# A hybrid decoder layer on one core: two accumulator tiles for each Strassen pair, weight casts 100 instructions sooner, and B and C of two groups computed as pairs

## The chip, the core and the metric

The kernel runs on one core of a Trainium2 chip. The metric is the device time of one execution in microseconds, and the median of several executions is what counts. The core's engines each work through their own queue of instructions in the order in which the program puts them: PE (TensorE: matmuls; PEld is its weight loads), DVE (VectorE), ACT (ScalarE), POOL (GpSimd, which here mostly issues DMAs and tiny copies) and SP (SyncE, which issues DMAs). They wait for each other through semaphores. An instruction whose wait isn't over holds up everything behind it on its engine.

## The reference, cut to what matters

One layer: a projection of the normalised input, a pooling branch and a Mamba-2 scan merged by gates, then an MLP. There are 512 tokens and 16 meta tokens ahead of them, so 528 positions, and 1024 channels. The lines that the change bears on:

```python
u = rmsnorm(h, mix_norm_w[i])
proj = u @ w_in[i]
u_pool = proj[..., OFF_POOL:OFF_Z]
z = proj[..., OFF_Z:OFF_XBC]
xbc = proj[..., OFF_XBC:OFF_DT]
...
xbc = jax.nn.silu(causal_depthwise_conv(xbc, conv_w, conv_b))
xs = xbc[..., :D_INNER]                                   # 8 groups of 256 columns
b_mat = xbc[..., D_INNER:D_INNER + SSM_GROUPS * D_STATE]  # 8 groups of 128
c_mat = xbc[..., D_INNER + SSM_GROUPS * D_STATE:]         # 8 groups of 128
...
y = ssd_chunked(xs, dt, a, b_mat, c_mat) + xs * d_skip[:, None]
y = y * jax.nn.silu(z)        # then a norm for each group, and w_ssd_out
```

So each of the eight groups of the scan needs two column blocks of x, one of B, one of C and two of z, each 128 columns wide: six products of a 1024 x 128 weight block with u.

## The kernel before, in words

**Numbers.** Every product is made in three passes, because each operand is split into a rounded high part and the remainder: high x high, high x low, low x high. For a weight block of 128 x 1024 numbers in float32 (`raw`), ACT casts it to `whi` (L111) and DVE subtracts to get `wlo` (L113); both stand in `block_split`. There are four buffers each for `whi` and `wlo`, and three for `raw` (one more of another pool during the scan). `block` (L115) allots the tiles, has SP load the block (`block_load`, L95) and splits it.

**A plain projection** (`proj`, L207, called by `plain` and `z_half`) multiplies the block with u: for x, B and C in two column runs of 264 (258 for C, whose leading positions aren't needed), 48 matmuls; for z and the gates 24 matmuls of 512 columns. `plain` accumulates in a tile of `psum2`, which has two buffers of two banks each; `conv` (L433) then reads it with one operation of ACT and three of DVE, and ends with a Silu on ACT.

**A pair** (`pair`, L492) computes two column blocks together in the Strassen-Winograd form: seven products of quarter blocks (`MULTIPLY`: `b11`, `b21`, `t2`, `t1`, `s3`, `b22`, `t4`), of 12 matmuls with 264 columns each, 84 in all, where two plain blocks need 96. Products `b11`, `t2`, `s3`, `t4` accumulate in the first bank, one on top of the other, `b21`, `t1`, `b22` in the second. After each product its state is copied or added to the raw result `r` in SBUF (L510 to L524, ACT and DVE by turns), and `conv` reads `r`. Before the change both banks are the halves of one `psum2` tile. The weights for four of the products are sums of quarter blocks; they are made beforehand in DRAM by POOL's DMAs, some of which add (`weight_steps`, L768). A set of sums covers two pairs. `pair_operands` (L471) loads two quarter products into one `raw` tile at a time and splits it with `block_split`, so a pair needs three and a half blocks' worth of casts and subtractions where two plain blocks need two. The right operands are sums of parts of u, made once by `sums_of_u` during groups 0 to 3. Before the change x is made as a pair in groups 4 to 7 (`X_PAIRS`), and B and C nowhere (`BC_PAIRS = ()`). A branch for B and C as pairs with z between them stands in `group_proj` and in the host's `_weight_blocks` under the name `both`, and is not taken.

**The weave.** `weave` (L728) writes the program for group g by turns: a step of the scan of group g (`ssd`, L590), a step of the projections of group g + 1 (`group_proj`, L529), a step of `sums_of_u` and a step of `weight_sums_at`, which issues one of POOL's DMAs behind a small copy of what was just written (`mark`). While group 4 is scanned, the first part of the output product (`out_half`) is woven in; beside group 7's scan runs `out_part`. In three weaves a gate (`gate_pool`) comes between x and z.

**The order.** The order of writing isn't the order of issue. A planner goes through the program with a model of the times and gives each engine, whenever it is free, the ready instruction that was written first. `tc.issue_after(x)` puts an instruction behind x on its engine; `tc.high_priority(100)` ranks the instructions written under it as if they had been written 100 instructions sooner. Tiles of a pool are handed out in the course of the plan: an instruction that needs a buffer waits for the release of the one before, by all its readers. The small accumulators `psum1` (four of one bank) serve the scan (`ptb`, `ptm`, `ptx`, `pcb`, `pst`, `po`, `py`, `png`); the two `psum2` tiles serve the projections.

**Sets of sums.** `sets` (L760) is the list of weight sums to make: first those of the pairs (`fx`, 8 DMAs each), then those of the MLP (`f1` with 8 DMAs, `f2` with 4). `SETS_AT` says how many sets each group's weave takes from the list; what is left is made behind the loads of `ht` (L1188), before the MLP.

Of the kernel before, what the change touches and what calls it, by code (L numbers as in the profile page):

```python
# [11 lines left out]
AF = mybir.ActivationFunctionType  # L12
# [4 lines left out]
SEQ = 512  # L17
NM = 16
L = SEQ + NM
HALF = L // 2  # L20
# [27 lines left out]
SUMS_AT = range(4)  # L48

X_PAIRS = (4, 5, 6, 7)  # L50
BC_PAIRS = ()
PAIRS = [(k, g) for g in range(G) for k in "bx" if g in (BC_PAIRS if k == "b" else X_PAIRS)]

SETS_AT = {0: 1, 1: 1, 2: 2, 3: 1, 4: 2, 5: 2, 6: 1, 7: 1}
# [10 lines left out]
def kernel(ctx: ExitStack, tc, xT, x, w, fx, f1, f2, vec, fnw, out):  # L65
    nc = tc.nc
    act, dve, pe, pool = nc.scalar, nc.vector, nc.tensor, nc.gpsimd
# [13 lines left out]
    def raw_tile(name):  # L81
        nraw[0] += 1
        if scan_raw and nraw[0] % 4 == 0:
            return scan_raw[0].tile([P, 1024], F32, tag="raw", name=name)
        return wp.tile([P, 1024], F32, tag="raw", name=name, bufs=3)
# [8 lines left out]
    def block_load(t, c):  # L94
        nc.sync.dma_start(t[1][:, c], w[t[0], :, c])  # L95
# [5 lines left out]
    def after(*ins):  # L101
        st = ExitStack()
        for i in ins:
            if i is not None:
                st.enter_context(tc.issue_after(i.ins))
        return st

    def block_split(t, c, behind=None, cast_behind=None):
        b, raw, hi, lo = t
        with after(cast_behind):  # L110
            act.copy(hi[:, c], raw[:, c])  # L111
        with tc.issue_after(behind.ins) if behind is not None else nullcontext():
            dve.tensor_tensor(lo[:, c], raw[:, c], hi[:, c].bitcast(F32), op=ALU.subtract)  # L113

    def block(behind=None, cast_behind=None):  # L115
        t = block_tiles()
        block_load(t, slice(0, 1024))
        block_split(t, slice(0, 1024), behind, cast_behind)
        return t[2:]

    def raw_block():
# [70 lines left out]
    def psum2(name):  # L192
        return psa.tile([P, 1024], F32, tag="mm", name=name)
# [55 lines left out]
    b = nblk[0]  # L249
# [102 lines left out]
    for i in range(2):  # L352
        pb = psum1(f"pb1_{i}")
        c = slice(3 * i, 3 * i + 3)
# [14 lines left out]
    for c in range(4):  # L369
        r = slice(c * H, (c + 1) * H)  # L370
# [19 lines left out]
    for c in (slice(0, P), slice(P, W)):  # L390
        n = c.stop - c.start
# [39 lines left out]
    x_ready, z_ready, filled = {}, {}, {}  # L431
# [39 lines left out]
    def pair_operands(i):  # L471

        s, h = divmod(i, 2)
        q = {"b11": B11, "b22": B22, "b21": B21}
        for a in range(0, 7, 2):
            ms = [m[0] for m in MULTIPLY[a : a + 2]]
            n = nblk[1]
            nblk[1] += 1
            raw = raw_tile(f"rawp{n}")
            hi = wp.tile([P, 1024], F32R, tag="whi", name=f"whip{n}")  # L480
            lo = wp.tile([P, 1024], F32R, tag="wlo", name=f"wlop{n}")
            for j, m in enumerate(ms):
                src = fx[s, q[m]] if m in q else wsum["fx", s, m]
                nc.sync.dma_start(raw[:, 512 * j : 512 * (j + 1)], src[:, 512 * h : 512 * (h + 1)])
            c = slice(0, 512 * len(ms))
            block_split((n, raw, hi, lo), c)
            for j in range(len(ms)):
                yield hi[:, 512 * j : 512 * (j + 1)], lo[:, 512 * j : 512 * (j + 1)]

    second_product, halved = {}, {}  # L490

    def pair(kind, g, r):  # L492

        ps = psum2(f"pq{kind}{g}")
        banks = (ps[:, :HALF], ps[:, 512 : 512 + HALF])
        operands = pair_operands(PAIRS.index((kind, g)))
        one, two = HF
        for m, f, n, start, stop in MULTIPLY:
            o = banks[n]
            wt = next(operands)  # L500
            f = factor_u(f)
            for low in range(2):
                for k in range(4):
                    wk = wt[low][:, k * P : (k + 1) * P]
                    at = pe.matmul(o, wk, f[k][0], start=start and not low and k == 0,  # L505
                                   stop=stop and low == 1 and k == 3, skip_group_check=True)
                    if not low:
                        pe.matmul(o, wk, f[k][1], start=False, stop=False, skip_group_check=True)
            if m == "b11":
                act.copy(r[0][:, one], o)  # L510
            elif m == "b21":
                dve.tensor_tensor(r[0][:, one], r[0][:, one], o, op=ALU.add)
            elif m == "t2":
                second_product[g] = at
                act.activation(r[1][:, one], o, AF.Copy, scale=-1.0)
            elif m == "t1":
                act.copy(r[1][:, two], o)
                yield
            elif m == "s3":
                dve.tensor_tensor(r[1][:, two], r[1][:, two], o, op=ALU.subtract)  # L520
            elif m == "b22":
                dve.tensor_tensor(r[1][:, one], r[1][:, one], o, op=ALU.add)
            else:
                act.copy(r[0][:, two], o)  # L524
# [4 lines left out]
    def group_proj(g, cur, gate=None):  # L529

        first = g == 0
        xc, bt, ct, zt = cur

        def plain(dst, t, skip):
            if first and (dst is bt or dst is ct):
                view = viewB if dst is bt else viewC
            else:
                runs, view = wide(psum2(f"px{g}_{t}"), skip)
                proj(runs, block(), X if first else U)
            conv(dst, first_raw(t, view, skip) if first else view, t)  # L540

        def z_half(ps, i):

            with tc.issue_after(done[0].ins) if g == 1 else nullcontext():
                wt = block(None, halved.get(g - 1) if gate is not None else None)
            proj(narrow(ps), wt, X if first else U, None if i else second_product.get(g))

        bcs = ((bt, 16 + g, 0), (ct, 24 + g, NM - 4))
        xs = ((xc[:, 0, :], 2 * g, 0), (xc[:, 1, :], 2 * g + 1, 0))
        both = g in BC_PAIRS  # L550
        for kind, ts, paired in (("b", bcs, both), ("x", xs, g in X_PAIRS)):
            if paired:
                r = raw_pair(kind, g)
                yield from pair(kind, g, r)
                for (dst, t, skip), src in zip(ts, r):
                    conv(dst, src[:, skip:], t)
                yield
            else:
                for t in ts:
                    plain(*t)  # L560
                    filled.setdefault(g - 1, mm[0])
                    yield
            if both:
                i = 0 if kind == "b" else 1
                ps = psum2(f"pz{g}_{i}")[:, :SEQ]
                z_half(ps, i)
                z_ready[g] = act.activation(zt[:, i, :], ps, AF.Silu)
                yield
        if both:
            return  # L570
        if gate is not None:
            gate_pool(gate)
            yield
        ps = psum2(f"pz{g}")
        for i in range(2):
            z_half(ps[:, i * SEQ : (i + 1) * SEQ], i)
        zf = zt.rearrange("p i t -> p (i t)")
        if first:
            dve.tensor_tensor(zt, ps.rearrange("p (i t) -> p i t", i=2),
                              rsb[:, NM:].unsqueeze(1).to_broadcast([P, 2, SEQ]), op=ALU.mult)  # L580
            z_ready[g] = act.activation(zf, zf, AF.Silu)
        else:
            z_ready[g] = act.activation(zf, ps, AF.Silu)
        yield
# [465 lines left out]
    for d in range(NK):  # L1050
        ps = psum1(f"psl{d}")
# [108 lines left out]
    for n, d in enumerate(MERGE):  # L1160
# [9 lines left out]
        ps = psum2(f"pup{d}")[:, :SEQ]  # L1170
# [389 lines left out]
    for c in range(NC - 1):  # L1560
        z, e = c == 0, c == NC - 2

        n = 2 * c + 3
        a = ff1_plain(n, (range(4), range(4, NK))) if n < PLAIN else ff1_pair(n)
        b = ff1_pair(n + 1) if n + 1 < 16 else iter(())
# [61 lines left out]
    c = NC - 1  # L1627
# [14 lines left out]
    for t in range(4):  # L1642
        T, st = t // 2, slice((t % 2) * P, (t % 2 + 1) * P)
        n = 0
        for half in range(2):
            parts = [(0, 512)] if half == 0 or t < 3 else [(0, 256), (256, 256)]
            for a, m in parts:
                ps = p2v[t] if T == 0 and half == 0 else lastp[:, 512:] if a else (
                    lastp[:, :512] if (t, half) == (3, 0) else psum1(f"pl{t}_{half}"))
                ps = ps[:, a : a + m]  # L1650
                i = 0
# [4 lines left out]
                for k, seg in ((1, (A11, 3)[T]), (0, (A12, A22)[T])):  # L1656
                    wh, wl = wq[k, half]
                    for p in range(2):
                        x0 = p * 512 + a
                        f = i == 0 and not (T == 0 and half == 0) and not a  # L1660
# [18 lines left out]
def _weight_blocks(i):  # L1679
# [14 lines left out]

    def group(g, gate_d=None):
        z = lambda j: put(cols(w_in, OFF_Z + (2 * g + j) * P))
        both = g in BC_PAIRS
        for i, ts in enumerate(((16 + g, 24 + g), (2 * g, 2 * g + 1))):
            if g not in (X_PAIRS if i else BC_PAIRS):
                for t in ts:  # L1700
                    put(cols(w_in, OFF_XBC + t * P))
            if both:
                z(i)
        if gate_d is not None:
            gate(gate_d)
        if not both:
            for j in range(2):
                z(j)

    def wg(b):  # L1710
        put(w_g[2 * b : 2 * b + 2].reshape(2, 2, P, 256).transpose(2, 0, 1, 3).reshape(P, 1024))
# [119 lines left out]
```

## Time and profile before

| | us |
|---|---|
| median of three runs | 1015.87 (1014.68 to 1016.35) |
| the profiled execution, its own time | 1013.97 |
| its span in the trace | 1012.3 |
| PE busy | 992.1 |
| DVE busy | 804.3 |
| ACT busy | 604.9 |
| POOL busy | 122.7 |

The program's own instructions fill the span; the profiled execution's own time has 1.67 us around it. Times in the trace are counted from the span's start. By the order of work the span divides roughly so: the first projections and gates until 72 us, the scan of groups 0 to 7 until about 480, pooling, gates and merging until 645, the output projection until 690, the MLP until the end. A row of a timeline gives start, length, engine, line, operation, what is written from what, the shape, how many were merged (x), and in brackets the engine's idle time before it and what ended that. A row of waits gives who waited for whom, the total, how often, and the longest. A row of a group of instructions ends with busy time, the mean in ns of one, and the idle time before them. PE's matmuls overlap, so the time that one costs is read from start to start.

### The profile page before, as it was taken

To read this page: it belongs to the slowest core of one execution; us is meant where nothing else is said; L and a number is where in the kernel's file an instruction comes from. 1 tells how busy PE (TensorE), PEld (TensorE's weight loads), DVE (VectorE), ACT (ScalarE), POOL (GpSimd) and SP (SyncE) were. 2 spreads that over 40 slices of the span, in tenths; PEclk is the share of its full clock that TensorE was granted. 3 is DMA by queue.
4 is the path that set the end of the run, shared out by engine and by line. 5 is a ranking of instruction groups with operands and counts; after the bars stand their busy time and mean duration, and the time that the engine had idled before them with its cause. 6 is when DMAs were issued, how large, how long until landed. Compare 5 with 4: busy or idle time off the path is not lost.

```text
span 1012.3 us, 15679 instructions
## 1 busy us (share of the span) xinstructions
PE 992.1 (98%) x6035; PEld 874.9 (86%) x6035; DVE 804.3 (79%) x1162; ACT 604.9 (60%) x856; POOL 122.7 (12%) x215
## 2 busy tenths in 40 slices
PE   9999997999999999999999999999999999999997
PEld 7889996988888898987899888887889999999986
DVE  7968896869853788978789657876988878888885
ACT  8657848395943666675445434367656656665654
POOL 0001221211112213213300000221000000000000
PEclk9999998999999999999999999999999999999999
DMA  7274877676889758587823631989354464554432
GB/s 255 85 259 128 252 217 188 180 196 189 232 244 262 207 147 255 137 264 156 270 84 124 230 125 62 288 199 337 91 187 150 142 195 138 166 172 151 137 105 84
DMA packets 61803, 184.52 MB, mean 182 GB/s; under 512 B 7072, under 2 KB 8416, under 8 KB 60704
## 3 DMA queue, kind: packets, MB, share of 16 engines
q1 hardware_dynamic: 39456, 109.00, 32.4%
q0 software_dynamic: 18240, 67.51, 26.1%
q10 hardware_dynamic: 4032, 7.00, 1.9%
q8 instruction: 47, 0.77, 0.3%
q14 instruction: 28, 0.23, 0.1%
HBM read 173.13 MB, written 58.59 MB: 229 GB/s over the span
## 4 chain that ended last, share of the span: by engine, by line
PE 90%; ACT 5%; DVE 2%; DMA 2%; issue 1%; ACTq 0%; DVEq 0%
PE px L1450 8%; PE px L214 7%; PE alpha L1518 6%; PE pz L214 6%; PE px L1453 4%; PE px L217 4%; PE alpha L1521 3%; PE pgp L214 3%; PE pz L217 3%; PE pgs L214 3%; PE pqx L505 3%; DMA raw<-in_w 2%; PE pso L145 1%; PE pgp L217 1%; PE pso L146 1%; PE pso L148 1%
## 5 line engine op out<-in xcount | busy, mean ns | idle before, releaser
L113 DVE TENSOR_TENSOR wlo<-raw,whi 128x1024 fp32r<-128x1024 f32 (+2 forms) x88 | 101.7, 1170 | 43.7 <-ACT whi L111 25.7
L111 ACT CAST whi<-raw 128x1024 fp32r<-128x1024 f32 (+2 forms) x88 | 87.5, 1010 | 74.8 <-DMA raw<-in_w 17.8
L214 PE MATMUL px<-uh,whi 128*128 128x264 f32 (+1 forms) x320 | 82.4, 295 | 5.7 <-ACT whi L111 5.7
L217 PE MATMUL px<-ul,whi 128*128 128x264 f32 (+1 forms) x320 | 79.9, 287 | 0.0
L214 PEld LDWEIGHTS px<-uh,whi 128*128 128x128 f32 x320 | 61.5, 192 | 7.1 <-ACT whi L111 6.0
L1225 DVE TENSOR_TENSOR ht<-ht,alpha 128x1024 f32<-128x1024 f32 x35 | 42.7, 1219 | 29.1 <-PE alpha L1518 29.1
L217 PEld LDWEIGHTS px<-ul,whi 128*128 128x128 f32 x320 | 61.3, 192 | 0.2
L1148 ACT CAST shi<-rawf 128x1024 fp32r<-128x1024 f32 x42 | 44.2, 1053 | 28.6 <-PE alpha L1521 18.2
L1518 PE MATMUL alpha<-shi,hh 128*128 128x512 f32 x140 | 55.2, 394 | 0.0
L1521 PE MATMUL alpha<-shi,hl 128*128 128x512 f32 x140 | 54.7, 391 | 0.0
L1149 DVE TENSOR_TENSOR slo<-rawf,shi 128x1024 fp32r<-128x1024 f32 x42 | 51.2, 1218 | 0.6 <-ACT shi L1148 0.6
L1453 PE MATMUL px<-vsl,shi 128*128 128x256 f32 x192 | 47.4, 280 | 0.0
L1450 PE MATMUL px<-vsh,shi 128*128 128x256 f32 x192 | 47.4, 281 | 0.0
L214 PE MATMUL pz<-uh,whi 128*128 128x512 f32 x112 | 43.9, 392 | 0.0
L217 PE MATMUL pz<-ul,whi 128*128 128x512 f32 x112 | 43.7, 390 | 0.0
L214 PE MATMUL px<-uh,wlo 128*128 128x264 f32 (+1 forms) x320 | 41.8, 283 | 0.0
L214 PEld LDWEIGHTS px<-uh,wlo 128*128 128x128 f32 x320 | 39.9, 188 | 0.0
L1518 PE MATMUL alpha<-slo,hh 128*128 128x512 f32 x140 | 37.4, 389 | 0.0
L1450 PEld LDWEIGHTS px<-vsh,shi 128*128 128x128 f32 x192 | 36.2, 188 | 0.9
L1453 PEld LDWEIGHTS px<-vsl,shi 128*128 128x128 f32 x192 | 36.1, 188 | 0.9
L1453 PE MATMUL px<-vl,shi 128*128 128x256 f32 x144 | 36.1, 283 | 0.0
L713 DVE RECIPROCAL rs<-rs 128x128 f32<-128x128 f32 x32 | 27.2, 911 | 11.1 <-ACT rs L711 10.9
(593 smaller groups left out, 3079.2 us busy)
## 6 DMA issues: line engine op xcount, KB each, us to landing
raw<-in_w SPq DMA_DIRECT2D x96, 512.0 KB, 4.7
f_t<-in_f POOLq DMA_DIRECT2D x38, 512.0 KB, 6.9
f_s<-in_f POOLq DMA_DIRECT2D x26, 512.0 KB, 6.6
b<-in_f SPq DMA_DIRECT2D x21, 512.0 KB, 4.5
rawf<-in_f SPq DMA_DIRECT2D x36, 256.0 KB, 3.0
rawf<-f_t SPq DMA_DIRECT2D x36, 256.0 KB, 3.2
abc<-acs_d POOLq DMA_DIRECT2D x8, 1024.0 KB, 6.5
f_t<-f_t POOLq DMA_DIRECT2D x12, 512.0 KB, 6.7
```

The lines of the kernel that those rows point to most:

```text
L111: act.copy(hi[:, c], raw[:, c])
L113: dve.tensor_tensor(lo[:, c], raw[:, c], hi[:, c].bitcast(F32), op=ALU.subtract)
L214: pe.matmul(o, wt, rhs[0][k][:, c], start=part == 0 and k == 0, stop=part == 1 and k == NK - 1)
L217: mm[0] = pe.matmul(o, wt, rhs[1][k][:, c], start=False, stop=False)
L505: at = pe.matmul(o, wk, f[k][0], start=start and not low and k == 0, stop=stop and low == 1 and k == 3, skip_group_check=True)
L1148: splits.append((act.copy(hi, src), dve.tensor_tensor(lo, src, hi.bitcast(F32), op=ALU.subtract)))
L1149: dve.tensor_tensor(lo, src, hi.bitcast(F32), op=ALU.subtract)))
L1225: added[0] = dve.tensor_tensor(o, o, src, op=op)
L1450: pe.matmul(ps, m, f[k][0], start=start and not low and k == 0, stop=stop and low == 1 and k == 3, skip_group_check=True)
L1453: pe.matmul(ps, m, f[k][1], start=False, stop=False, skip_group_check=True)
L1518: pe.matmul(ps[t], hh[:, p, seg, st], m, start=bool(first and not low and p == 0), stop=bool(last and low and p == 1), skip_group_check=True)
L1521: pe.matmul(ps[t], hl[:, p, seg, st], m, start=False, stop=False, skip_group_check=True)
```

## The change

It has three parts.

1. `pair` accumulates in two tiles, one of `psum2` and one of `psum1`, in place of the two halves of one `psum2` tile.
2. `block` (load, cast and subtraction) and the `block_split` in `pair_operands` are written under `tc.high_priority(100)`. The loads of the pairs' quarters, `pool_pair`'s `split_form`, `out_part`'s own casts and the MLP's `split` are not.
3. `BC_PAIRS = (5, 6)`: B and C of groups 5 and 6 are computed as pairs. The list of pairs becomes x4, b5, x5, b6, x6, x7, so three sets `fx` in place of two, and all later sets move back by one place. The branch `both` goes. `filled`, behind which the product C B^T (`pcb`) of the group before is issued, becomes the end of `t2` of the B and C pair where there is one; `second_product[g]` is set by both pairs of a group, and z is issued behind the later one. The host no longer puts B's and C's plain blocks of these groups into `in_w`, and lays their quarters into `in_fx`.

```diff
-BC_PAIRS = ()
+BC_PAIRS = (5, 6)
 PAIRS = [(k, g) for g in range(G) for k in "bx" if g in (BC_PAIRS if k == "b" else X_PAIRS)]
...
     def block(behind=None, cast_behind=None):
         t = block_tiles()
-        block_load(t, slice(0, 1024))
-        block_split(t, slice(0, 1024), behind, cast_behind)
+        with tc.high_priority(100):
+            block_load(t, slice(0, 1024))
+            block_split(t, slice(0, 1024), behind, cast_behind)
         return t[2:]
...
             c = slice(0, 512 * len(ms))
-            block_split((n, raw, hi, lo), c)
+            with tc.high_priority(100):
+                block_split((n, raw, hi, lo), c)
...
     def pair(kind, g, r):
 
-        ps = psum2(f"pq{kind}{g}")
-        banks = (ps[:, :HALF], ps[:, 512 : 512 + HALF])
+        banks = (psum2(f"pq{kind}{g}")[:, :HALF], psum1(f"po{kind}{g}")[:, :HALF])
...
-        both = g in BC_PAIRS
-        for kind, ts, paired in (("b", bcs, both), ("x", xs, g in X_PAIRS)):
+        for kind, ts, paired in (("b", bcs, g in BC_PAIRS), ("x", xs, g in X_PAIRS)):
             if paired:
                 r = raw_pair(kind, g)
-                yield from pair(kind, g, r)
+                for _ in pair(kind, g, r):
+                    filled.setdefault(g - 1, second_product[g])
+                    yield
                 for (dst, t, skip), src in zip(ts, r):
                     conv(dst, src[:, skip:], t)
                 yield
...
-            if both:
-                i = 0 if kind == "b" else 1
-                ps = psum2(f"pz{g}_{i}")[:, :SEQ]
-                z_half(ps, i)
-                z_ready[g] = act.activation(zt[:, i, :], ps, AF.Silu)
-                yield
-        if both:
-            return
```

More of the change, by code (lines that the diff above doesn't have):

```diff
@@ L1696, in group @@
         z = lambda j: put(cols(w_in, OFF_Z + (2 * g + j) * P))
-        both = g in BC_PAIRS
         for i, ts in enumerate(((16 + g, 24 + g), (2 * g, 2 * g + 1))):
@@ L1701, in group @@
                     put(cols(w_in, OFF_XBC + t * P))
-            if both:
-                z(i)
         if gate_d is not None:
             gate(gate_d)
-        if not both:
-            for j in range(2):
-                z(j)
+        for j in range(2):
+            z(j)
     def wg(b):
```

## The prediction

> **What bounds the kernel now.** I read the page's busy times first, then TensorE's own waits, then windows and timelines around the longest of them. PE is the engine to watch.
>
> ```profile
> span 1012.3 us, 15679 instructions
> PE 992.1 (98%) x6035; PEld 874.9 (86%) x6035; DVE 804.3 (79%) x1162; ACT 604.9 (60%) x856; POOL 122.7 (12%) x215
> PE px L214 <- ACT whi L111: 5.7, 1, 5.7
> PE pqx L505 <- DVE rax L512: 1.5, 1, 1.5
> PE pqx L505 <- ACT rax L510: 1.4, 1, 1.4
> ```
>
> PE is idle for 1012.3 - 992.1 = 20.2 us of the span. So nothing but fewer matmuls or shorter waits of PE can shorten the kernel, and waits have at most 20.2 us to give, part of it at the two ends. One wait is 5.7 us, for a weight cast. Two more stand inside a pair (L505). These are the three places where the change acts.
>
> The long wait lies where the weave of group 2 begins (163.9 us):
>
> ```profile
> 165.00:170.00 5.00, 0.52 (x5) 0.28 (x3) 2.35 (x4) 4.96 (x7) 1.38 (x3) 0.78 0.72 125
> 170.00:175.00 5.00, 3.75 (x18) 3.75 (x19) 3.77 (x4) 4.04 (x5) 0.00 (x0) 0.54 0.54 173
> 175.00:180.00 5.00, 5.00 (x42) 4.96 (x41) 1.92 (x2) 1.84 (x2) 0.00 (x0) 1.00 0.89 315
> 150.24 2.00 ACT L111 CAST whi<-raw 128x1024 fp32r<-128x1024 f32 x2
> 168.26 1.06 ACT L644 ACTIVATE abc<-abc 128x1024 f32<-128x1024 f32 x1
> 169.22 1.04 ACT L643 ACTIVATE abc<-abc 128x1024 f32<-128x1024 f32 x1
> 170.17 3.87 ACT L111 CAST whi<-raw 128x1024 fp32r<-128x1024 f32 x4
> 164.48 1.04 PE L618 MATMUL ptx<-ident,xc 128*128 128x128 f32 x8
> 171.25 0.59 PE L214 MATMUL px<-uh,whi 128*128 128x264 f32 x1 [5.73 <-ACT whi L111]
> 171.64 0.42 PE L217 MATMUL px<-ul,whi 128*128 128x264 f32 x1
> 174.50 0.34 PE L214 MATMUL px<-uh,whi 128*128 128x264 f32 x1
> ```
>
> The columns of a window are its stretch and length, then busy us of PE, PEld, DVE, ACT and POOL, the granted clock, the DMA share and GB/s. ACT is busy 4.96 of 5 us while PE has 0.52: ACT works through the exponentials of the scan (L643, L644) and casts weights only at 170.17. There it runs four casts back to back (3.87 us), so all four `whi` buffers were free and the blocks loaded; only the order on ACT held the first one. After the wait PE runs at half pace: 13 steps from 171.64 to 174.50 take 2.86 us, 0.22 us each, with a granted clock of 0.54 in that window.
>
> **The change, part by part.** *Casts sooner.* The cast that ends the wait needs about 1 us (the two at 150.24 take 2.00). Put ahead of L644 and L643, or further ahead, it is done before the last `ptx` at 165.5. That removes up to 5.73 us of idle time and the slow clock after it. A normal step is 0.12 us (below: 5.71 us for 48), so the slow clock costs 13 x 0.10 + the first matmul's 0.3 = 1.6 us. The exponentials come 1 to 4 us later; their readers are the products of `py`, which stand behind two 5.8 us blocks of PE, so that delay is covered here. What the casts cost elsewhere: an engine's instructions run in their planned order, so a cast or its subtraction (DVE) in front of a reader of PSUM holds the bank. The narrowest such place is group 0's weave:
>
> ```profile
> 89.03 0.94 PE L684 MATMUL po<-ct,st 128*128 128x128 f32 x6 [0.87 <-DVE st L672]
> L113 DVE TENSOR_TENSOR wlop<-rawp,whip 128x1024 fp32r<-128x1024 f32 (+1 forms) x4 | 4.3, 1086 | 2.2 <-PE pz L214 2.2
> L111 ACT CAST whip<-rawp 128x1024 fp32r<-128x1024 f32 (+1 forms) x4 | 3.8, 938 | 2.7 <-PE px L217 2.7
> ```
>
> PE waits for DVE there already, so one subtraction more ahead of it is paid in full: 1.2 us (1.086 is the mean over half and full blocks). Bounds: 0 and, with two blocks ahead, 2.4; I take 1.2.
>
> [...]
>
> *Two accumulator tiles.* Both halves of a pair's result lay in one tile, and a matmul into one half waited for the reader of the other:
>
> ```profile
> 240.00:245.00 5.00, 2.96 (x30) 2.47 (x29) 5.00 (x11) 3.21 (x5) 1.54 (x3) 1.00 0.48 188
> 242.53 0.39 PE L505 MATMUL pqx<-uh,whip 128*128 128x264 f32 x1 [1.40 <-ACT rax L510]
> 244.92 0.50 PE L214 MATMUL pgp<-uh,whi 128*128 128x512 f32 x1 [0.65 <-ACT whi L111]
> 338.81 0.39 PE L505 MATMUL pqx<-t0h,whip 128*128 128x264 f32 x1 [1.50 <-DVE rax L512]
> 242.09 0.38 ACT L510 COPY rax<-pqx 128x264 f32<-128x264 f32 x1
> 335.14 0.38 ACT L510 COPY rax<-pqx 128x264 f32<-128x264 f32 x1
> 243.82 1.05 ACT L111 CAST whi<-raw 128x1024 fp32r<-128x1024 f32 x1 [1.35 <-PE pqx L508]
> ```
>
> At 242.53 the product `b21` (second bank) waits for L510, the copy out of the first bank; at 338.81 `t2` (first bank) waits for L512, which reads the second. With two tiles `b21` starts at once and `t2` needs only L510, done at 335.5. Both waits go: 1.40 + 1.50. The 0.65 us at 244.92 filled such a wait with a gate's product whose cast came late; with `t2` free to follow `b21`, it is not needed there. Sum 3.55 us, taken as 3.5; bounds 2.9 and 3.55. The second tile takes one of the four one-bank tiles from `b21` to `b22`, so `po`, `py`, `pst` of the scan share three. The scan uses them in turn, and PE has products between, so I put 0 on it here and count it with the new pairs.
>
> *B and C of groups 5 and 6 as pairs.* One plain block and one product of a pair, group 5's:
>
> ```profile
> 327.76 0.28 PE L214 MATMUL px<-uh,whi 128*128 128x258 f32 x1
> 331.55 2.08 PE L214 MATMUL px<-uh,wlo 128*128 128x258 f32 x16
> 333.47 0.28 PE L505 MATMUL pqx<-uh,whip 128*128 128x264 f32 x1
> 334.94 0.49 PE L605 MATMUL ptb<-ident,bt 128*128 128x128 f32 x3
> ```
>
> C's block of 48 matmuls takes 333.47 - 327.76 = 5.71 us; B's has 264 columns for 258, so 5.71 x 264 / 258 = 5.84. A product of a pair takes 334.94 - 333.47 = 1.47; seven are 10.29. Saved: 11.55 - 10.29 = 1.26 a group, 2.5 for both; with a few tenths for seven starts in place of two I take 2.3. On the other engines a pair casts 3.5 blocks for 2 and empties seven products: 1.5 x 1.05 + 4 x 0.38 = 3.1 us more on ACT and about as much on DVE. Their cover is the stage they fall in:
>
> ```profile
> 362.80:405.70 42.90, 42.87 (x310) 38.87 (x310) 35.11 (x50) 27.32 (x40) 8.62 (x17) 1.00 0.66 204
> 112.20:163.90 51.70, 51.70 (x358) 47.03 (x358) 45.40 (x77) 37.39 (x55) 12.14 (x20) 1.00 0.75 218
> 446.32 0.83 POOL L782 DMA_DIRECT2D f_t<-f_t  x1 [5.14 <-DMA f_t<-in_f]
> rawp<-in_fx SPq DMA_DIRECT2D x12, 256.0 KB, 5.7
> rawf<-in_f SPq DMA_DIRECT2D x36, 256.0 KB, 3.0
> ACT whi L111 <- DMA raw<-in_w: 17.8, 7, 4.8
> ```
>
> Group 5's weave (362.8 to 405.7) has DVE at 35.1 of 42.9 and would have 38; ACT 30. It fits on average, not at every hand-over. Each new pair has six hand-overs of a bank; I take one subtraction's length, 1.2 us, for each pair, 2.4 in all (bounds 0 and 5.0).
>
> Six pairs in place of four make a third set of summed weights: eight more copies of 512 KB on POOL's queue in group 2, which pushes every later set back. Group 2 and group 5 issue 12 copies for 8, groups 3 and 6 issue 4 for 8, group 7 issues 8 for 4, and five sets for four remain behind the loads of `ht`. Behind them on POOL stand the loads of `abc` and, in group 7, the additions to `acc_d` and the reloads of `acc`. A copy that waits for another's landing can cost 5.14 us (446.32). The sums move behind other work and are due groups later, so I take 0; the upper end, 5.1, stays in the range.
>
> Sum: -5.7 - 1.6 - 3.5 - 2.3 = -13.1, and +1.2 + 2.4 = +3.6: **-9.5 us**. The profiled execution took 1013.97 us (span 1012.3 and 1.67 around it), so 1004.5. The median of the runs is 1015.87, 1.90 above that execution: **1006.4 us**.
>
> **The rivals.** *A, slower: subtractions in front of the scan.* DVE has 45.4 of 51.7 us in group 1's weave (row 112.20). If each of the seven hand-overs between groups puts two subtractions (2 x 1.22) ahead of the reads that free `px` and `pst`, PE loses 7 x 2.44 = 17.1 us and the sum is -13.1 + 17.1 = +4, or 1020. It decides from six of seven hand-overs on (13.1 / 2.44 = 5.4). For it: the wait at 89.03. Against it: the subtractions are the same in number, and four `whi` buffers bound how far they run ahead.
>
> *B: the casts don't move where it counts.* A hundred instructions may not reach past the exponentials, or a buffer isn't free (243.82 waited 1.35 us for PE). Then only -3.5 - 2.3 + 2.4 = -3.4 stays: 1012.5. Four casts in a row at 170.17 speak against it.
>
> *C: the transfers come late.* The same 256 KB land in 5.7 us during the scan and in 3.0 in the MLP. Casts placed sooner wait at the head of ACT for their load, as they do now for 17.8 us in seven places, and hold what is behind. If two loads of each new pair and two at each of the two heavier groups (2 and 5) are exposed by that difference, that is 8 x 2.7 = 21.6 us at worst and half of it, 10.8, with cover for every second: -9.5 + 10.8 = +1.3, 1017. Against it: a DMA share of 0.66 in group 5. [...]
>
> **How the numbers follow.** My forecast 0.54; B 0.15; A 0.16; C 0.15. Faster by over 0.2% (2 us, what a measurement of this kernel can tell from no change) holds the forecast and nearly all of B, 0.68; C is split between no change and slower, so 0.08 the same and 0.24 slower. The likeliest case's own range is 1002.8 (no loss) to 1011 (5.1 us of landing besides). For 8 in 10 it reaches over B and C and to the near part of A: 1001.5 to 1018.
>
> **What would show it.** Right: the 5.73 us wait and the clock of 0.54 near 165 us are gone; no PE wait names L510 or L512 from the other bank; about 24 matmuls fewer; and group 5's and group 6's weaves shorter by a us each. Wrong: new PE waits above 1 us for L439, L672 or a cast in groups 0 to 3 (A), the wait at 165 still there (B), or `raw` and `rawp` landings ending PE's or ACT's waits (C).

## The result and the profile after

| | us |
|---|---|
| before, median of 8 runs beside the changed kernel | 1014.72 (1012.99 to 1016.35) |
| after, median of 8 runs | 1019.01 (1017.65 to 1020.5) |
| ratio after / before | 1.0041, 95% interval 1.003 to 1.0052 |
| after: the profiled execution, its own time and its span | 1020.5 and 1018.8 |

The kernel is slower by 0.4%, where 1006.4 us was forecast and 1018 was the upper end. First the page of the changed kernel, its span and PE's busy time, against the two lines of before:

```profile
span 1018.8 us, 15687 instructions
PE 993.0 (97%) x6011; PEld 877.2 (86%) x6011; DVE 810.1 (80%) x1172; ACT 608.6 (60%) x867; POOL 125.0 (12%) x227
```

24 matmuls fewer, as they should be, and still PE is busy 0.9 us longer and idle for 25.8 us in place of 20.2. PE's waits of the changed kernel say where (who waits for whom, total, how often, longest):

```profile
PE ptb L599 <- ACT bt L442: 5.7, 1, 5.7
PE pqb L506 <- ACT rab L511: 5.4, 1, 5.4
PE pz L991 <- ACT pu L1003: 1.9, 1, 1.9
PE pz L215 <- DVE xc L440: 1.7, 1, 1.7
PE pqx L506 <- ACT rax L511: 1.4, 1, 1.4
```

The 5.7 us for a cast (`px` behind `whi`) has gone from the list, and so have both waits of a pair for a copy or addition on its other bank (the 1.4 us of `pqx` above, in weave 5, is a wait for the copy out of the bank that the product itself adds onto). The window where that cast was late shows PE full at the full clock in the changed kernel:

```profile
165.00:170.00 5.00, 5.00 (x45) 5.00 (x43) 5.00 (x13) 4.99 (x12) 1.53 (x3) 1.00 0.86 215
170.00:175.00 5.00, 5.00 (x38) 4.79 (x37) 3.07 (x5) 4.97 (x7) 0.00 (x0) 1.00 0.78 238
```

In its place stand two waits of the same size, at 327 and 358 us, and both lie at the new pairs.

To find all of the difference I cut each span at the first `ptm` transpose of each group, so that a piece is the scan of group g with the projections of group g + 1 in it (a weave); weave 7 ends at the first `psl` matmul. Lengths in us, from the trace of one profiled execution each. The third row is the first experiment below: the change without its third part.

| kernel | to 0 | 0 | 1 | 2 | 3 | 4 | 5 | 6 | 7 | rest |
|---|---|---|---|---|---|---|---|---|---|---|
| before | 71.0 | 44.4 | 48.9 | 56.0 | 49.7 | 87.7 | 42.7 | 42.6 | 55.0 | 514.3 |
| after | 71.0 | 45.7 | 48.5 | 38.1 | 58.6 | 91.9 | 49.6 | 42.5 | 58.8 | 514.1 |
| after, no B and C pairs | 70.5 | 45.7 | 48.5 | 38.1 | 58.6 | 85.2 | 41.8 | 42.4 | 54.5 | 514.3 |

Weaves 2 and 3 together are 9.0 us shorter than before: the old wait, and the pair's wait at 242.53. Weaves 4, 5 and 7 are 4.2, 6.9 and 3.8 us longer, and that is more. Against the kernel without the new pairs they are 6.7, 7.8 and 4.3 longer, 18.8 of the 19.0 us between the two spans (1018.8 and 999.8). (The traced execution of the changed kernel is the slowest of its eight, the other one next to the fastest of its four, so by the medians it is less, see below.) Weaves 4 to 7 as windows of the changed kernel (stretch, length, busy us of PE, PEld, DVE, ACT and POOL, granted clock, DMA share, GB/s):

```profile
261.90:353.80 91.90, 86.23 (x491) 75.55 (x490) 55.29 (x78) 46.27 (x67) 17.25 (x33) 0.96 0.83 231
353.80:403.40 49.60, 42.83 (x299) 39.65 (x298) 37.09 (x59) 30.75 (x46) 8.80 (x18) 0.93 0.68 197
403.40:445.90 42.50, 42.45 (x311) 39.06 (x310) 36.21 (x59) 26.97 (x41) 10.68 (x21) 1.00 0.79 209
445.90:504.70 58.80, 55.06 (x306) 46.03 (x305) 45.27 (x68) 33.81 (x50) 20.02 (x33) 0.97 0.85 218
```

and of the kernel without the new pairs:

```profile
261.40:346.60 85.20, 85.20 (x502) 74.65 (x501) 52.12 (x73) 43.78 (x61) 18.90 (x34) 1.00 0.90 259
346.60:388.50 41.90, 41.82 (x311) 38.82 (x310) 34.19 (x54) 27.13 (x40) 8.67 (x16) 1.00 0.66 197
430.90:485.50 54.60, 52.98 (x307) 44.84 (x306) 44.36 (x67) 33.65 (x49) 15.71 (x24) 1.00 0.83 199
```

Without them PE has not a tenth of a microsecond of idle time in weaves 4 and 5. With them, weave 5 has 6.8 us idle (49.6 - 42.83), and its clock is at 0.93: 23 matmuls ran in a stretch at 0.50 (last section). Weave 6, which makes only the x pair as before, does not change.

**Weave 5, group 6's pair.** The timeline of the changed kernel, PE first, then ACT:

```profile
354.80 0.37 PE L506 MATMUL pqb<-uh,whip 128*128 128x264 f32 x1
357.29 0.65 PE L506 MATMUL pob<-uh,wlop 128*128 128x264 f32 x4
363.29 0.59 PE L506 MATMUL pqb<-t0h,whip 128*128 128x264 f32 x1 [5.36 <-ACT rab L511]
...
353.66 1.03 ACT L577 ACTIVATE zt<-pz 128x1024 f32<-128x1024 f32 x1 [1.19 <-PE pz L215]
354.58 0.58 ACT L601 COPY btok<-ptb 128x512 f32<-128x512 f32 x1
355.18 1.28 ACT L626 ACT_TABLE_LOAD   x1
356.47 2.14 ACT L626 ACTIVATE eb<-abc 64x1024 f32<-64x1024 f32 x2
358.64 2.44 ACT L631 ACTIVATE abc<-abc,dtok 128x128 f32<-128x128 f32 x8
360.99 1.04 ACT L638 ACTIVATE abc<-abc 128x1024 f32<-128x1024 f32 x1
361.93 1.04 ACT L637 ACTIVATE abc<-abc 128x1024 f32<-128x1024 f32 x1
362.88 0.35 ACT L511 COPY rab<-pqb 128x264 f32<-128x264 f32 x1
```

PE makes `b11` and `b21`, 3.1 us of work. The third product, `t2`, adds onto the bank of `b11`, so it needs the copy L511 first. ACT is not idle: from 353.66 on it runs without a gap through the work that opens a group's scan (z's Silu, a table load, the exponentials), and the copy, ready at about 356.5, comes last, at 362.88. The same place in the kernel without the new pairs:

```profile
347.65 0.37 PE L215 MATMUL px<-uh,whi 128*128 128x264 f32 x1
351.64 2.09 PE L215 MATMUL px<-uh,wlo 128*128 128x264 f32 x16
353.57 1.06 PE L649 MATMUL pcb<-ct,bt 128*128 128x128 f32 x8
354.89 1.46 PE L658 MATMUL pst<-xdd,btok 128*128 128x256 f32 x6
356.00 0.47 PE L215 MATMUL px<-uh,whi 128*128 128x258 f32 x1
355.64 0.77 ACT L437 ACTIVATE bt<-px,vs 128x528 f32<-128x528 f32 x1
```

The same burst of ACT is there, and PE does not notice: B's plain block, whose cast is done before, needs nothing from ACT for 5.9 us, then `pcb` and `pst` take 2.4, and C's block goes to the other `px` tile. A pair gives ACT its first copy after 1.5 us and needs it done after 3.1. Two plain blocks were not only work, they were the cover for the opening of the scan.

**Weave 4, group 5's pair.** The timeline of the changed kernel where the other wait lies, ACT and PE in order of time:

```profile
327.57 1.05 ACT L111 CAST whi<-raw 128x1024 fp32r<-128x1024 f32 x1 [1.97 <-DMA raw<-in_w]
...
330.87 1.28 ACT L442 ACT_TABLE_LOAD   x1 [1.54 <-DVE bt L440]
332.17 0.64 ACT L442 ACTIVATE bt<-bt 128x528 f32<-128x528 f32 x1
332.72 0.36 ACT L511 COPY rax<-pqx 128x264 f32<-128x264 f32 x1
332.87 0.48 PE L599 MATMUL ptb<-ident,bt 128*128 128x128 f32 x1 [5.67 <-ACT bt L442]
```

Here two pairs follow each other, B and C's and then x's. On ACT a cast waits 1.97 us for its load and the table load 1.54 for a tap of B's convolution, and only then come B's Silu and the copy. PE has done `b11` and `b21` of the x pair and stops from 327.2 to 332.87. The page names the Silu of B, but the copy of x's `b11`, for which the next product of the pair waits, stands right behind it on ACT. B and C come out of their pair together, so both convolutions (the taps on DVE, L440) and their Silus come at once, and z, the only other work PE could do, is held behind the x pair's third product (L547, `second_product`).

**Weave 7.** The third set of sums moves an `f1` set with eight DMAs to where an `f2` set with four stood. POOL, then ACT and PE, in the changed kernel:

```profile
484.80 0.83 POOL L776 DMA_DIRECT2D f_t<-f_t  x1 [4.58 <-DMA f_t<-in_f]
485.60 0.59 ACT L861 COPY sp<-psp 128x512 f32<-128x512 f32 x1 [6.52 <-DMA acc_d<-sp]
498.89 1.04 ACT L111 CAST whi<-raw 128x1024 fp32r<-128x1024 f32 x1 [2.99 <-DMA raw<-in_w]
499.84 0.37 ACT L1003 COPY pu<-pz 128x264 f32<-128x264 f32 x1
500.26 0.39 PE L991 MATMUL pz<-t1h,whiB 128*128 128x264 f32 x1 [1.86 <-ACT pu L1003]
```

POOL waits 4.58 us for a copy to land before it can add to it; behind it stand the additions to `acc_d`, for which ACT's copies into `sp` wait; a cast further on waits for its load, and behind the cast stands the copy L1003 for which PE waits (1.86 us). The rows don't show whether that load is late because of POOL's copies. Behind the wait the granted clock is 0.50 for 3.41 us (last section), which costs about 1.7 us more: the wait and the slow clock together are 3.6 of this weave's 4.3 us.

### The profile page after: what moved, and what is told of

Its sections match the earlier page's. It is cut to its first block, busy times and chain, and to the rows that moved or that the text cites. A ratio compares the mean times of both kernels' runs of the same rounds, so it can differ in the third digit from the quotient of the medians.

```text
span 1018.8 us, 15687 instructions
## 1 busy us (share of the span) xinstructions
PE 993.0 (97%) x6011; PEld 877.2 (86%) x6011; DVE 810.1 (80%) x1172; ACT 608.6 (60%) x867; POOL 125.0 (12%) x227
## 4 chain that ended last, share of the span: by engine, by line
PE 88%; ACT 5%; DMA 3%; DVE 3%; issue 1%; SPq 0%; POOL 0%; ACTq 0%; DVEq 0%; POOLq 0%
PE px L1444 8%; PE alpha L1512 6%; PE px L215 6%; PE pz L215 6%; PE px L1447 4%; PE alpha L1515 3%; PE pgp L215 3%; PE pz L218 3%; PE px L218 3%; PE pgs L215 3%; PE pqx L506 2%; PE pgp L218 1%; PE pso L146 1%; DMA raw<-in_w 1%; PE py L684 1%; PE wo_alpha L1206 1%
## 5 line engine op out<-in xcount | busy, mean ns | idle before, releaser
L113 DVE TENSOR_TENSOR wlo<-raw,whi 128x1024 fp32r<-128x1024 f32 (+2 forms) x84 | 97.3, 1169 | 39.1 <-ACT whi L111 29.8
L111 ACT CAST whi<-raw 128x1024 fp32r<-128x1024 f32 (+2 forms) x84 | 83.0, 1009 | 57.8 <-DMA raw<-in_w 14.6
L1219 DVE TENSOR_TENSOR ht<-ht,alpha 128x1024 f32<-128x1024 f32 x35 | 42.7, 1220 | 29.2 <-PE alpha L1512 29.2
L215 PE MATMUL px<-uh,whi 128*128 128x264 f32 (+1 forms) x256 | 65.2, 292 | 0.0
L218 PE MATMUL px<-ul,whi 128*128 128x264 f32 (+1 forms) x256 | 63.2, 285 | 0.0
L215 PEld LDWEIGHTS px<-uh,whi 128*128 128x128 f32 x256 | 48.3, 189 | 1.0 <-issue 0.9
L218 PEld LDWEIGHTS px<-ul,whi 128*128 128x128 f32 x256 | 48.2, 188 | 0.3 <-issue 0.2
L113 DVE TENSOR_TENSOR wlop<-rawp,whip 128x1024 fp32r<-128x1024 f32 (+1 forms) x24 | 26.1, 1086 | 25.3 <-PE pso L149 7.7
L111 ACT CAST whip<-rawp 128x1024 fp32r<-128x1024 f32 (+1 forms) x24 | 22.6, 944 | 27.7 <-PE pso L147 11.7
L1444 PE MATMUL px<-vh,shi 128*128 128x256 f32 x144 | 36.0, 282 | 0.0
```

Of the source, the lines that this page charges most:

```text
L215: pe.matmul(o, wt, rhs[0][k][:, c], start=part == 0 and k == 0, stop=part == 1 and k == NK - 1)
L218: mm[0] = pe.matmul(o, wt, rhs[1][k][:, c], start=False, stop=False)
L1219: added[0] = dve.tensor_tensor(o, o, src, op=op)
L1444: pe.matmul(ps, m, f[k][0], start=start and not low and k == 0, stop=stop and low == 1 and k == 3, skip_group_check=True)
```

## The experiments

**The parts one by one.** Four kernels on one chip, beside before at 1013.62 us. First, the changed kernel with the third part taken out:

```diff
-BC_PAIRS = (5, 6)
+BC_PAIRS = ()
```

> The changed kernel with BC_PAIRS = () (two tiles and sooner casts stay). Theory M (the new B and C pairs make the loss: PE has to wait for ACT and DVE after nearly every product of such a pair, where two plain blocks ran for 11.5 us without them): the waits of 5.7 and 5.4 us (ptb, pqb) are gone, and the wait near 165 us of the kernel before stays gone: 7.3 + 3.5 = 10.8 us under the kernel before, some 1004 (1002 to 1008). Rival K (the sooner casts and subtractions crowd ACT and DVE and delay the scan): the loss stays without the pairs, no faster than the kernel before, 1014 or more.

Measured 1002.79 us, 0.9886 of before (0.9868 to 0.9905). So the third part costs what the other two bring and more: 1.0041 / 0.9886 is 1.6%, 16 us by the runs, and 19.0 by the two profiled executions.

Before, with the priority alone:

```diff
-        block_load(t, slice(0, 1024))
-        block_split(t, slice(0, 1024), behind, cast_behind)
+        with tc.high_priority(100):
+            block_load(t, slice(0, 1024))
+            block_split(t, slice(0, 1024), behind, cast_behind)
...
-            block_split((n, raw, hi, lo), c)
+            with tc.high_priority(100):
+                block_split((n, raw, hi, lo), c)
```

> The kernel before with sooner casts alone. Theory M: the 5.7 us wait near 165 us and the slow clock behind it go, 7.3 us, and the pair's own waits stay: 1007.5 (1005 to 1010). Rival K: slower than the kernel before, 1016 or more, with new waits for conv or state updates on DVE.

Measured 1010.46 us, 0.9962 (0.9947 to 0.9977). Weaves 2 and 3 are 6.8 us shorter than before (98.9 against 105.7), but weave 4 is 2.6 longer (90.3): a pair's wait on its other bank grew from 1.5 to 2.6 us there, and the granted clock of the weave is 0.98. The list of PE's waits of this kernel (total, how often, longest):

```profile
PE pqx L507 <- DVE rax L514: 3.3, 2, 2.6
```

Before, with the two tiles alone:

```diff
-        ps = psum2(f"pq{kind}{g}")
-        banks = (ps[:, :HALF], ps[:, 512 : 512 + HALF])
+        banks = (psum2(f"pq{kind}{g}")[:, :HALF], psum1(f"po{kind}{g}")[:, :HALF])
```

> The kernel before with two accumulator tiles alone. Both theories: the waits for L510 and L512 from the other bank go, 2.9 to 3.5 us, the wait near 165 us stays: 1011.5 (1010 to 1013). If the second tile takes a one-bank tile that the scan needs, there are new waits of po or py and no gain, 1014 or more.

Measured 1008.22 us, 0.9939 (0.9921 to 0.9958). The two weaves with a pair's wait are 2.6 (weave 3) and 2.5 us (weave 4) shorter, more than the 1.4 and 1.5 of the waits themselves.

The changed kernel without the priority (the first edit of the two above undone):

> The changed kernel without the sooner casts (two tiles and the pairs of B and C stay). Theory M: the wait near 165 us comes back and the two new waits stay, so slower than the changed kernel by some 7 us: 1026 (1021 to 1029). Rival K: faster than the changed kernel, 1014 or less, and the two new waits are gone.

Measured 1024.67 us, 1.0112 (1.0091 to 1.0133). The old wait of 5.7 us is back, and the new ones stay (5.5 and 4.3 us in the list of waits). So the new waits don't come from casts ranked sooner.

**What in the third part costs it.** Four kernels on another chip, beside before at 1014.99 us. The sums: the third set is left out, and the x pairs of groups 6 and 7 are computed from the second set's sums, so the MLP's sets stand again where they stood before. The result of this kernel is not the layer's.

```diff
-                src = fx[s, q[m]] if m in q else wsum["fx", s, m]
+                src = fx[s, q[m]] if m in q else wsum["fx", min(s, 1), m]
...
-    sets = [("fx", n) for n in range(fx.shape[0])] + [
+    sets = [("fx", n) for n in range(2)] + [
```

> The changed kernel without the third set of weight sums: eight copies of POOL are left out, every later set is back at its old place, and the last two pairs use the second set's sums in place of their own. Theory M (PE waits for ACT and DVE inside the new pairs): the waits of ptb and pqb stay at 5 us or more, the weaves of groups 4 and 5 stay within 1 us of the changed kernel's 91.9 and 49.6; only group 7's weave, where eight copies stand in place of four, falls from 58.8 towards 55: 1015 (1013 to 1017). Rival D (the additional transfers make the loss): both waits shrink below 2 us, 1009 or less.

Measured 1016.99 us, 1.0016 (1.0005 to 1.0027). Weave 7 falls from 58.8 to 55.1 us, PE's wait there from 1.9 to 0.3. The other two waits stay at 5.3 us each, with eight transfers fewer: they don't come from the third set's transfers.

Group 6's B and C alone as a pair:

```diff
-BC_PAIRS = (5, 6)
+BC_PAIRS = (6,)
```

> B and C as a pair in group 6 alone. Theory M: group 5's share (some 7 us in group 4's weave) goes, group 6's stays (49 us for 42 in group 5's weave, with the wait of pqb for L511), and so does the shift of the sums: 1002.8 + 7.8 + 4.3, some 1014 (1011 to 1017). If the loss comes from two such pairs together, less than half of it stays: 1009 or less.

Measured 1013.85 us, 0.9988 (0.9974 to 1.0001). Weave 4 is back at 85.2 us, weave 5 stays at 50.0 with its wait of 5.2, weave 7 is at 60.5. The two pairs' losses are separate.

z no longer held behind the x pair's third product:

```diff
-            proj(narrow(ps), wt, X if first else U, None if i else second_product.get(g))
+            proj(narrow(ps), wt, X if first else U, None if i or g in BC_PAIRS else second_product.get(g))
```

> The changed kernel with z of groups 5 and 6 no longer issued behind the pair's product t2, so that the plan puts 19 matmuls of z between b21 and t2 of group 5's x pair, where PE waited; group 6's first pair still has nothing in that place. Theory M (PE has no other work while ACT and DVE are behind): group 4's weave falls by 4 to 6 us, group 5's stays at 49 or more with the pqb wait of 5 us: 1014 (1012 to 1016). Rival T (ACT and DVE are short of throughput there, so filling only moves the wait): no gain, 1018 or more.

Measured 1013.66 us, 0.999 (0.9977 to 1.0003). Weave 4 is at 86.0 us: part of z's first half fills the place of the wait. In weave 5 the wait stays at 5.5 us.

The pair's copies and casts ranked 200 instructions sooner, so that the order on ACT and DVE changes and no work is added or left out:

```diff
-            with tc.high_priority(100):
+            with tc.high_priority(200):
                 block_split((n, raw, hi, lo), c)
...
+            with tc.high_priority(200):
                 if m == "b11":
                     act.copy(r[0][:, one], o)
```

> The changed kernel with the copies out of a pair's banks (L511 to L525) and the pair's casts written 200 instructions sooner, so that in the plan they stand between the exponentials of the scan and no longer behind all of them. Theory M in the form that ACT's order makes the wait: pqb's wait for L511 falls from 5.4 to under 1.5 us, group 5's weave from 49.6 to 43 or 44, and group 4's wait for bt shrinks too: 1009 (1006 to 1013). Rival T: the exponentials, later by what was put before them, stop py instead, and the total stays at 1017 or more.

Measured 1014.37 us, 0.9992 (0.9979 to 1.0005). Weave 5 falls from 49.6 to 41.9 us, the length it has with plain blocks: the copy now stands between the two `eb` exponentials, and no product of B and C's pair waits (one of x's waits 0.7 us). So the copy's place in ACT's order makes that wait. Weave 4 improves only to 89.7, and this kernel's timeline there shows something new:

```profile
329.48 0.76 DVE L440 SCALAR_TENSOR_TENSOR bt<-rab,vs,bt 128x525 f32<-128x525 f32 x1
330.32 0.38 ACT L512 COPY rax<-pqx 128x264 f32<-128x264 f32 x1 [3.37 <-DVE bt L440]
330.75 0.59 PE L506 MATMUL pqx<-t0h,whip 128*128 128x264 f32 x1 [4.40 <-ACT rax L512]
```

The copy is first in line on ACT, and ACT stands idle 3.37 us for the last tap of B's convolution, which ends at 330.24. That tap reads `rab`; `rax` has the same buffer, since the pool gives each of the two raw results one buffer. So in weave 4 the second pair can't empty its first bank before the first pair's convolution is done, however the engines are ordered. This is read from the rows and the kernel; no run gave the raw results a second pair of buffers. Weave 6 has got longer here (47.9 us for 42.5), which gives back most of what weave 5 won.

**Work put under the waits.** Two kernels on another chip, beside before at 1015.91 us. In the change, the scan's product C B^T (`pcb`, and behind it the state products `pst`) is issued behind the pair's `t2`, the product that waits. Here it is released one product sooner, by `b21`:

```diff
             elif m == "b21":
+                second_product[kind, g] = at
                 dve.tensor_tensor(r[0][:, one], r[0][:, one], o, op=ALU.add)
...
-                    filled.setdefault(g - 1, second_product[g])
+                    filled.setdefault(g - 1, second_product[kind, g])
```

> After the change, with the product C B^T of the scan (and so the state products behind it) released by the end of the B and C pair's second product b21 in place of its third, t2. If the 5.4 us wait in group 5's weave is long because the pair leaves PE nothing else to do while ACT works through the exponentials, these 14 matmuls (2.4 us in the kernel without B and C pairs) now stand inside it: the wait for the copy falls from 5.4 to about 3.0 us, group 5's weave from 49.6 to about 47, or to about 44 if 3 us of idle time no longer bring the slow clock; the whole to 1014 to 1017. Group 4's wait of 5.7 us and its weave (91.9) stay. If PE's idle time there is set by the transfers or by the chain of bank readers alone, the wait stays above 5 us and the whole at 1019.

Measured 1017.27 us, 1.0016 (1.0001 to 1.0031). The timeline of PE in weave 5, and a window of it:

```profile
358.02 1.05 PE L650 MATMUL pcb<-ct,bt 128*128 128x128 f32 x8
358.91 0.60 PE L657 MATMUL pst<-xddm,btok 128*128 128x256 f32 x2
359.35 1.46 PE L659 MATMUL pst<-xdd,btok 128*128 128x256 f32 x6
363.52 0.39 PE L506 MATMUL pqb<-t0h,whip 128*128 128x264 f32 x1 [2.72 <-ACT rab L511]
```

```profile
360.00:365.00 5.00, 2.28 (x16) 1.86 (x15) 2.11 (x2) 4.68 (x10) 0.00 (x0) 1.00 0.21 86
```

The wait is 2.72 us in place of 5.36, the clock stays at 1.00, and weave 5 falls from 49.6 to 45.3. So this wait was long for want of other work. Weave 7 took 61.0 us in this profile, which gives 2.2 of the 4.3 back, and the interval of the runs just touches that of the change (1.003 to 1.0052): that this wait got shorter is shown by the trace.

The same with z free as above:

> The same release of C B^T by b21, and z of groups 5 and 6 not held behind the x pair's third product as well. If the two waits each need only other work of PE to be covered, group 4's weave is at about 86 and group 5's at about 44 to 47, and the whole about 2 to 5 us below the kernel with z free alone, 1009 to 1012. If the two edits take the same work for cover, group 5's weave stays at 47 to 50 and the whole at 1014.

Measured 1009.47 us, 0.993 (0.9903 to 0.9956): weave 4 at 85.9, weave 5 at 44.9. The two edits cover two different waits.

**The causes mended together, and the best version.** Two kernels on a fourth chip, beside before at 1014.55 us. The first keeps the new pairs, with z of group 5 free, the copies and casts of groups 5 and 6 ranked 200 sooner as above, and no set of sums in weave 7:

```diff
-SETS_AT = {0: 1, 1: 1, 2: 2, 3: 1, 4: 2, 5: 2, 6: 1, 7: 1}
+SETS_AT = {0: 1, 1: 1, 2: 2, 3: 1, 4: 2, 5: 2, 6: 1, 7: 0}
```

> The changed kernel with all three losses treated: z of group 5 free to run beside its x pair, the copies and casts of the pairs of groups 5 and 6 written 200 instructions sooner, and no set of sums in group 7's weave. Theory M: no PE wait above 2 us in the weaves of groups 4 to 7, their lengths no more than 1 us over those without B and C pairs (85.2, 41.8, 42.4, 54.5): 1003 (1000 to 1007), so that the pairs at best come out even. If the 24 matmuls fewer count in full, 1000.5. If another cost of the pairs was overlooked, 1009 or more.

Measured 1006.9 us, 0.9926 (0.9906 to 0.9945). Weaves 4, 5 and 7 are at 85.0, 42.6 and 55.1 us. Three edits take back 1.15 of the 1.6% (1.0041 - 0.9926). It is still 0.4% above the kernel without the pairs; most of that is weave 6, 45.5 us for 42.4, where this kernel's list of waits has two new rows (the second one's cause the profile doesn't show):

```profile
PE po L680 <- DVE st L668: 1.3, 1, 1.3
PE py L686 <- issue: 1.3, 1, 1.3
```

The kernel with the copies first has both rows too (1.5 and 1.2 us), and weave 6 of every other kernel is at most 43.1 us, so they go with the earlier ranking.

The second is the kernel without the pairs, with that last line of sums taken out too:

> The two first parts of the change without pairs of B and C, and without a set of sums in group 7's weave (its four copies come after the loads of ht). If POOL's copies cost something there even at four (group 7's weave 54.5 us), 1001; otherwise as without this edit, 1002.8 (1001 to 1004).

Measured 1002.38 us, 0.9878 (0.9857 to 0.9898), the same as 0.9886 within the intervals: with the sets in their old order, the runs show no cost of weave 7's sums. Parts one and two alone, at 1002 to 1003 us, are the fastest kernel of the study.

## Why the prediction was wrong

**The casts: right.** The wait at 165 us and the slow clock behind it (0.54 from 170 to 175 us before, 1.00 in the changed kernel) went as said, worth 7.3 us in the sum; with the two tiles in both, weaves 2 and 3 take 96.7 us with the priority and 104.1 without, 7.4 less. The loss of 1.2 was right in size too: weave 0 takes 45.7 us for 44.4, and PE waits 1.7 us once for a convolution with a subtraction between its taps (`pz` for `xc` in the list). It was put at the scan's `po`, and came at z's projection.

**The two tiles: right in kind, too small.** 3.5 us with bounds 2.9 and 3.55; the tiles alone brought 5.4 by the runs (1013.62 to 1008.22) and 4.5 by the spans. The waits as they stood in one plan were taken as all there was to gain. With the casts moved as well, the old shared tile would have cost more (3.3 us in the kernel with the priority alone), so the two parts together bring 10.8 us (1013.62 to 1002.79), where they bring 3.2 and 5.4 one at a time. The forecast for both, without the third part's terms, was 13.1 - 2.3 - 1.2 = 9.6.

**The new pairs: the step that failed.** "Each new pair has six hand-overs of a bank; I take one subtraction's length, 1.2 us, for each pair, 2.4 in all (bounds 0 and 5.0)." It took the cover from averages: "It fits on average, not at every hand-over." Measured against the kernel without the pairs, weaves 4 and 5 lose 14.5 us (6.7 + 7.8), where the step with the saving of 2.3 beside it said about none. Not many small hand-overs, but one in each group, the first for which the copy of a `b11` is needed (group 5's x, group 6's B and C), and each took 5.4 to 5.7 us with a clock of 0.50 for 6.83 us from inside the wait on (330.85 to 337.68 and 361.57 to 368.40). What the prediction passed over was the cover that the removed work gave: two plain blocks are 11.5 us of PE's time that needs nothing from ACT once their casts are made. In weave 5 they stood exactly where ACT is busy without a gap for 9 us. In weave 4 the cause is another, the second of two pairs in a row: it can't empty its first bank before the first pair's convolution is done. The row of the burst (L643, L644, then the casts, after 168.26) was in the prediction, read only as the reason for the old wait. The releases written in the diff (`filled` and z behind `second_product`) then kept PE from the work that could have stood in.

**The matmuls saved: the count was right, the time wasn't there.** 24 fewer at 0.12 us (5.71 us for 48) is 2.9 us, against the 2.3 taken. But even with the wait gone, weave 5 with a pair takes 41.9 us and with plain blocks 41.8. The windows agree: PE is busy 41.82 of 41.90 us without pairs, and in the kernel with the copies first

```profile
350.80:392.60 41.80, 40.85 (x298) 37.52 (x297) 36.70 (x59) 30.38 (x46) 11.93 (x16) 1.00 0.74 211
```

so the microsecond saved in matmuls is lost in idle gaps, 0.7 us of them the wait of x's pair.

**The sums on POOL: mis-sized.** "The sums move behind other work and are due groups later, so I take 0; the upper end, 5.1, stays in the range." 3.7 us in weave 7 (58.8 to 55.1 with the third set left out), within the bounds, at one of the places that the prediction named: the additions to `acc_d` behind a copy that waits 4.58 us for a landing. The size is that of one trace each; over the traces of all fourteen kernels, weave 7 takes 54.5 to 56.5 us with four copies or none in it, and 56.6 to 61.0 with eight.

**The rivals.** A (subtractions ahead of the scan) cost 1.3 us at one hand-over between groups, not at six. B fell with the wait at 165. C, late transfers, gave nearly the right time, 1017, for another reason: it put the loss on `raw` and `rawp`, and both new waits stay at 5.3 us when the third set's transfers are left out, while the ranking of copies and casts alone removes one of them. In weave 4 a cast does wait 1.97 us for its load; DVE's taps, for which ACT then waits, were held up by ACT for 0.24 us only (row 329.37 of DVE's timeline), and what more the load may have added isn't shown. None of the rivals was the one that happened, a wait for ACT's copy in place of the one for ACT's cast.

## What to carry to other kernels

Before work is taken off the busiest engine, ask what it covers: here a block of 5.9 us that needs nothing from the other engines hid ACT's burst, and a shorter form with a hand-over every 1.5 us did not, however much room the average showed. Price each new hand-over at the longest unbroken run of the engine that serves it at that place, not at the length of one instruction, ask which buffer it needs empty, and look for what the waiting engine may do meanwhile, which the new order may forbid. When a change has parts, measure each alone and all but one: here two gained 1.1% and the third lost 1.6%.

## What the runs showed of the hardware

In these traces the slow clock doesn't follow from the length of a wait alone: 5.36 us of idle time went with 6.83 us of it, 5.46 us with 3.3, 2.85 us with 3.4, and 2.72 us with none. First the changed kernel, with its stretches at 0.50 at the waits of 5.36 us (weave 5) and 1.86 us (weave 7) as windows:

```profile
361.57:368.40 6.83, 5.11 (x23) 5.12 (x24) 1.66 (x2) 3.31 (x6) 0.00 (x0) 0.50 0.22 74
501.52:504.93 3.41, 3.41 (x17) 3.41 (x17) 2.52 (x5) 1.90 (x2) 2.41 (x5) 0.50 1.02 351
```

The first stretch begins inside the wait, and PE is busy for 5.11 us of it, so it costs about 2.6 us; the second costs about 1.7. In the second a matmul of 264 columns starts every 0.22 us (502.08 to 503.84 in PE's timeline), and every 0.12 us just before it (500.49 to 501.35). Now the same place in weave 5 in other kernels, as windows of 5 us. The kernel with z free, after 5.46 us:

```profile
357.00:362.00 5.00, 4.78 (x28) 4.78 (x29) 1.65 (x2) 2.18 (x4) 0.00 (x0) 0.67 0.27 88
```

The kernel with z free and `pcb` released sooner, after 2.85 us:

```profile
355.00:360.00 5.00, 2.68 (x16) 2.68 (x17) 2.96 (x3) 3.88 (x7) 0.00 (x0) 0.84 0.11 43
360.00:365.00 5.00, 5.00 (x35) 4.83 (x35) 3.24 (x6) 1.33 (x2) 0.00 (x0) 0.82 0.31 105
```

A clock of 0.67 over 5 us is 3.3 us at 0.50, and 0.84 and 0.82 together are 3.4 (0.16 and 0.18 of 5 us, doubled), if the low clock is the 0.50 of the changed kernel here too. The 2.72 us of the kernel with `pcb` released alone brought none (1.00 in its window above and in the 5 us behind it). So nearly the same idle time went with 6.83 us of slow clock or with 3.3 (5.36 and 5.46 us), and with 3.4 or none (2.85 and 2.72); and 1.86 us came before 3.41 us of it. What decides between them, these rows don't show.
